# The scale of the first 128 channels as 16 single-column products on TensorE

## The chip, the cores and the metric

The kernel runs on one core of one Trainium2 chip. The metric is the device time of one execution in microseconds (us). Engines: PE is TensorE's matmul, PEld its weight load, DVE is VectorE, ACT is ScalarE, POOL is GpSimd, SP is SyncE, whose queue issues most DMAs.

## The reference

One layer of a bidirectional encoder, float32, with SEQ = 1024 positions, D = 2048 channels, batch 1. Only mixer 0, the pooling mixer, is used at this depth.

```python
m = silu(c) @ w_mod + b_mod                  # c: (1, D); shift, scale, gate of D each
shift, scale, gate = split(m, 3)
h = rms_norm(x) * (1.0 + scale) + shift
u, g = split(h @ w_in, 2)                    # w_in: (D, 2 D)
pooled = [centred_window_mean(u_i, w) - u_i  for w in (2, 4, 8, 16)]   # four groups of 512 channels
y = (pooled @ w_grp) * pool_scale
x = x + gate * ((y * silu(g)) @ w_out)
out = rms_norm(x) * final_norm_g
```

## The kernel before, in words

Activations lie with channels on partitions: x is given transposed (`xT`), so a block k of 128 channels is a tile of 128 x 1024. There are 16 such blocks, k = 0 to 15. Each large product is made from three: both operands are split into a high part in the type fp32r (`whi`, `hhi`) and a low part, the difference to it (`wlo`, `hlo`), and PE does high x high, low x high and high x low.

The first loop (lines 249 to 274) goes over k. For each k it needs three loads: 128 rows of the modulation matrix, given transposed so that output channels lie on partitions (`wm`, 1 MB), 128 rows of x (`xs`, 512 KB) and a block of weights of 128 x 512 (`wraw`, 256 KB). VectorE multiplies `wm` with SiLU(c) and sums along the row; that is the scale of these 128 channels (`mss[:, k, 1]`, after adding `b_mod` and 1, tile `bss`). For this, c is loaded as a copy over all partitions (`cB`, 128 x 2048, 1 MB), on which ScalarE does SiLU in two halves. For k = 0 to 3 the dot product is made in two halves of 1024 (`first_scale`, line 238), for later k in one (`mod_dot`, line 191). ScalarE then makes `hhi` = x times the scale (line 254; two halves for k < 4), VectorE makes `hlo` (`low_half`, line 226), and PE does 24 products of 128 x 512 into four pairs of PSUM banks `g_ps` (`first_products`, line 230). The factor of the RMS norm is applied later: ScalarE squares x (line 256), VectorE sums the squares in `acc` (`add_square`).

The order of the work is the order of the code: the schedule is written by hand, each engine works through its instructions in that order, and SP issues loads in that order. A new tile for `wm`, of which there are three buffers, waits until the last reader of its buffer is done.

Before the loop the loads go out in this order: the copy of c in two halves, `bss`, `wm` of k = 0 in two halves, `wraw` of k = 0, x of k = 0 in two halves, then `wm`, x and `wraw` of k = 1 and of k = 2. PE meanwhile does N_WARM = 30 products of a tile of ones into a bank that nobody reads (`warm`, line 219).

After the first loop come the other products with the input weights (line 170), the group products, the shift, the output products (line 878) and the closing norm. Where a sum over channels is needed, the kernel uses products with a single column of ones: 8 of them for the sum of squares (line 709) and others for the shift (`shift_sum`, line 331).

Of the kernel before, what the change touches and what calls it, by code (L numbers as in the profile page):

```python
# [8 lines left out]
F32 = mybir.dt.float32  # L9
F32R = mybir.dt.float32r  # L10
AF = mybir.ActivationFunctionType
ALU = mybir.AluOpType
PSUM = bass.MemoryType.PSUM
DRAM = bass.MemoryType.DRAM

N_WARM = 30
P = 128
D = 2048
T = 1024
NK = D // P  # L20
# [4 lines left out]


@with_exitstack
def encoder_layer(ctx, tc, xT, x, c, mod_ss, mod_g, b_ss, b_g, w_steps, wo_steps, pool_scale, edge_rcp, final_g, out):
    nc = tc.nc
    const = ctx.enter_context(tc.tile_pool(name="const", bufs=1))  # L30
    psum = ctx.enter_context(tc.tile_pool(name="psum", bufs=1, space=PSUM))
# [7 lines left out]
    bss = const.tile([P, NK, 2], F32, name="bss")  # L39
    mss = const.tile([P, NK, 2], F32, name="mss")  # L40
# [97 lines left out]
    modp = tc.alloc_tile_pool(name="modp", bufs=1, side="right")  # L138
# [4 lines left out]
    def row_tile(slot, name):  # L143
        return upool.tile([P, T + 2 * PAD], F32, tag=f"row{slot}", name=name)
# [4 lines left out]
    def load(s):  # L149
        if s < n_steps:  # L150
            w_raw[s] = wpool.tile([P, 512], F32, tag="wraw", name=f"wraw{s}")
            nc.sync.dma_start(out=w_raw[s], in_=w_steps[s])
# [22 lines left out]
    with tc.manual_schedule():  # L175

        cB = modp.tile([P, D], F32, name="cB")
        wm, xs, sq = {}, {}, {}

        def load_mod(i, k, parts=1):  # L180
            wm[i, k] = modp.tile([P, D], F32, tag="wm", bufs=3, name=f"wm{i}_{k}")
            w = D // parts
            for t in range(parts):
                nc.sync.dma_start(out=wm[i, k][:, t * w:(t + 1) * w], in_=mod_ss[i, k * P:(k + 1) * P, t * w:(t + 1) * w])
# [11 lines left out]
        def mod_bias(i, k):  # L196
            nc.vector.tensor_tensor(out=mss[:, k, i:i + 1], in0=mss[:, k, i:i + 1], in1=bss[:, k, i:i + 1], op=ALU.add)

        for t in range(2):
            nc.sync.dma_start(out=cB[:, t * 1024:(t + 1) * 1024], in_=c[:, t * 1024:(t + 1) * 1024].broadcast_to([P, 1024]))  # L200
        nc.sync.dma_start(out=bss, in_=b_ss)
        load_mod(1, 0, 2)
        load(0)
        xs[0] = row_tile(0, "x0")[:, :T]
        for t in range(2):
            nc.sync.dma_start(out=xs[0][:, t * 512:(t + 1) * 512], in_=xT[0:P, t * 512:(t + 1) * 512])
        for k in (1, 2):
            load_mod(1, k, 2)
            load_x(k)
            load(k)  # L210
        for t in range(2):
            nc.scalar.activation(cB[:, t * 1024:(t + 1) * 1024], cB[:, t * 1024:(t + 1) * 1024], AF.Silu)

        h_hi, h_lo = {}, {}

        warm, warm_in = bank_pair(3, "warm"), upool.tile([P, 512], F32R, tag="row4", name="warm_in")
        nc.vector.tensor_copy(out=warm_in.rearrange("p (a b) -> p a b", a=4), in_=ones.rearrange("p (o b) -> p o b", o=1).broadcast_to([P, 4, P]))
        for n in range(N_WARM):
            nc.tensor.matmul(warm[:, 0, :], warm_in[:, 0:P], warm_in, start=True, stop=True)
        g_ps = [bank_pair(j, f"g_ps{j}") for j in range(4)]  # L220

        def add_square(k):
# [15 lines left out]
        def first_scale(k):  # L238

            m = wm.pop((1, k))  # L240
            for t in range(2):
                a = slice(t * 1024, (t + 1) * 1024)
                nc.vector.tensor_tensor_reduce(out=m[:, a], in0=m[:, a], in1=cB[:, a], scale=1.0, scalar=0.0, op0=ALU.mult, op1=ALU.add, accum_out=mg[:, t, k:k + 1])
            if k == 0:
                nc.vector.tensor_scalar(out=bss[:, :, 1], in0=bss[:, :, 1], scalar1=1.0, scalar2=None, op0=ALU.add)
            nc.vector.scalar_tensor_tensor(out=mss[:, k, 1:2], in0=mg[:, 0, k:k + 1], scalar=mg[:, 1, k:k + 1], in1=bss[:, k, 1:2], op0=ALU.add, op1=ALU.add)

        first_scale(0)
        for k in range(NK):
            if k > 3:  # L250
                mod_bias(1, k)
            h_hi[k] = hpool.tile([P, T], F32R, tag="hi", bufs=NK, name=f"hhi{k}")
            for a in [slice(0, T)] if k > 3 else [slice(0, 512), slice(512, T)]:
                nc.scalar.activation(h_hi[k][:, a], xs[k][:, a], AF.Copy, scale=mss[:, k, 1:2])
            sq[k] = row_tile(3 + k % 2, f"sq{k}")[:, :T] if k else acc
            nc.scalar.activation(sq[k], xs[k], AF.Square)
            split_hi(k + 1)
            split_lo(k)
            if k < 3:
                low_half(k)  # L260
            add_square(k - 1)
            if k < 3:
                first_scale(k + 1)
            elif k + 1 < NK:
                mod_dot(1, k + 1)
            if k >= 3:
                low_half(k)
            if k + 3 < NK:
                load_mod(1, k + 3, 2 if k == 0 else 1)
            else:  # L270
                load_mod(0, k + 3 - NK)
            load_x(k + 3)
            load(k + 3)
            first_products(k)
# [341 lines left out]
        for s in range(NK, n_steps):  # L616
# [75 lines left out]
            if q == 0 or kind == "grp":  # L692
                name = f"{job[0]}{job[1]}_{job[2]}"
                ps = take_pair(name)
            hi, lo = w_hl.pop(s)
            for i in range(4):
                if s == sum_at and i == 2:
                    early_sum()
                a = slice(i * P, (i + 1) * P)
# [340 lines left out]
```

## Time and profile before

| | |
|---|---|
| median of 3 runs | 1136.46 us |
| lowest, highest run | 1133.23, 1136.73 us |
| profiled execution: its time | 1137.46 us |
| profiled execution: its span, first to last instruction | 1135.7 us |
| mean granted clock of TensorE | 0.993 |
| PE busy | 1118.6 us, 98% |
| PEld busy | 921.7 us, 81% |
| DVE busy | 729.8 us, 64% |
| ACT busy | 320.4 us, 28% |
| HBM read, written | 205.59 MB, 60.83 MB |

All stretches are counted from the first instruction of the span. The busy time of an engine says how full it is over the whole span; what a change in one stage is worth is read from the chain of waits and from the time line of that stage. Products are pipelined on PE: the next begins before the one ahead has ended, so the time per product is read from the starts of groups, not from the mean duration of one. In a count of a short stretch, products that only reach into it are counted too. The granted clock is 1.00 at 2.4 GHz and 0.50 at 1.2 GHz.

### The profile page before, as it was taken

Reading aid. Unit: us, or ns where it says so; the run is one execution under the profiler, and the core shown is the slowest. Engines: PE = TensorE matmul, PEld = TensorE weight load, DVE = VectorE, ACT = ScalarE, POOL = GpSimd, SP = SyncE. Lnnn points to the kernel's source line nnn. Section 1 sums busy time; section 2 is a strip of 40 time slices with the busy share of each in tenths; the row PEclk is TensorE's granted clock in tenths of the full one; section 3 lists DMA queues with packets and bytes.
Section 4 is the critical chain, followed back from the end, with each engine's and each line's share of the span. In section 5 each row is a group of like instructions: output and inputs, shape, how many; then the busy total and the mean of one; then the engine's idle time right before and its main releaser. Section 6 shows DMA issues by size and latency. Waiting matters only on the chain.

```text
span 1135.7 us, 13202 instructions
## 1 busy us (share of the span) xinstructions
PE 1118.6 (98%) x4938; PEld 921.7 (81%) x4938; DVE 729.8 (64%) x1218; ACT 320.4 (28%) x444; POOL 38.7 (3%) x79
## 2 busy tenths in 40 slices
PE   9999999999999999999999999999999999999996
PEld 7888887788888888888887888888888888888886
DVE  6996877866655566665646477634355358477795
ACT  4544110331221111222102112211235345242453
POOL 0000000000000000000000000000000010002100
PEclk9999999999999999999998999999999999999998
DMA  9995889147958977735797311123396667649954
GB/s 367 369 354 218 326 299 275 63 148 223 267 141 239 308 213 235 204 86 151 242 253 222 117 47 47 55 84 102 121 330 227 211 178 269 202 165 242 243 194 193
DMA packets 86335, 233.72 MB, mean 206 GB/s; under 512 B 9088, under 2 KB 17280, under 8 KB 82432
## 3 DMA queue, kind: packets, MB, share of 16 engines
q1 hardware_dynamic: 78464, 205.63, 51.8%
q0 software_dynamic: 7808, 27.27, 13.4%
q8 instruction: 38, 0.62, 0.2%
q14 instruction: 25, 0.20, 0.1%
HBM read 205.59 MB, written 60.83 MB: 235 GB/s over the span
## 4 chain that ended last, share of the span: by engine, by line
PE 84%; DMA 8%; DVE 6%; issue 1%; ACT 1%; SPq 0%; DVEq 0%; ACTq 0%
PE ops L878 26%; PE ps_u L170 23%; PE ps_g L170 20%; PE ps_y L170 8%; PE g_ps L235 6%; DMA gm<-in_mod_g 3%; DVE wm L194 3%; DMA early<-in_w_steps 2%; DMA wm<-in_mod_ss 1%; PE ops L972 1%; DMA wraw<-in_w_steps 1%; DMA gdram<-gr 1%; DVE wlo L162 1%; DVE early_acc L432 1%; PE vs_ps L331 0%
## 5 line engine op out<-in xcount | busy, mean ns | idle before, releaser
L162 DVE TENSOR_TENSOR wlo<-wraw,whi 128x512 fp32r<-128x512 f32 x144 | 99.2, 689 | 195.2 <-ACT whi L156 195.0
L156 ACT CAST whi<-wraw 128x512 fp32r<-128x512 f32 x144 | 89.1, 620 | 327.2 <-DMA wraw<-in_w_steps 105.8
L170 PE MATMUL ps_u<-hhi,wlo 128*128 128x512 f32 x512 | 158.4, 391 | 2.5 <-DVE wlo L162 2.5
L170 PE MATMUL ps_u<-hhi,whi 128*128 128x512 f32 x512 | 159.9, 394 | 0.0
L170 PE MATMUL ps_u<-hlo,whi 128*128 128x512 f32 x512 | 158.4, 390 | 0.0
L878 PE MATMUL ops<-wohi,zhi 128*128 128x512 f32 x432 | 133.0, 389 | 0.0
L878 PE MATMUL ops<-wohi,zlo 128*128 128x512 f32 x432 | 133.0, 389 | 0.0
L878 PE MATMUL ops<-wolo,zhi 128*128 128x512 f32 x432 | 132.9, 389 | 0.0
L170 PE MATMUL ps_g<-hhi,whi 128*128 128x512 f32 x384 | 119.9, 394 | 1.6 <-ACT whi L156 1.6
L170 PE MATMUL ps_g<-hhi,wlo 128*128 128x512 f32 x384 | 119.7, 393 | 1.2 <-DVE wlo L162 1.2
L170 PE MATMUL ps_g<-hlo,whi 128*128 128x512 f32 x384 | 119.2, 392 | 0.0
L170 PEld LDWEIGHTS ps_u<-hhi,wlo 128*128 128x128 f32 x512 | 96.2, 188 | 23.5 <-DVE wlo L162 3.3
L568 DVE TENSOR_TENSOR wolo<-woraw,wohi 128x1024 fp32r<-128x1024 f32 x56 | 68.4, 1221 | 72.7 <-ACT wohi L567 72.3
L170 PEld LDWEIGHTS ps_u<-hlo,whi 128*128 128x128 f32 x512 | 96.6, 189 | 20.4
L170 PEld LDWEIGHTS ps_u<-hhi,whi 128*128 128x128 f32 x512 | 95.7, 189 | 19.9 <-issue 0.5
L878 PEld LDWEIGHTS ops<-wohi,zhi 128*128 128x128 f32 x432 | 81.1, 188 | 16.9
L878 PEld LDWEIGHTS ops<-wolo,zhi 128*128 128x128 f32 x432 | 81.1, 188 | 16.8
L878 PEld LDWEIGHTS ops<-wohi,zlo 128*128 128x128 f32 x432 | 81.1, 188 | 16.8
L170 PEld LDWEIGHTS ps_g<-hhi,wlo 128*128 128x128 f32 x384 | 72.8, 190 | 17.0 <-DVE wlo L162 1.7
L170 PEld LDWEIGHTS ps_g<-hhi,whi 128*128 128x128 f32 x384 | 72.3, 190 | 16.8 <-ACT whi L156 2.0
L170 PEld LDWEIGHTS ps_g<-hlo,whi 128*128 128x128 f32 x384 | 72.6, 189 | 15.4
L567 ACT CAST wohi<-woraw 128x1024 fp32r<-128x1024 f32 x56 | 58.9, 1051 | 55.5 <-DVE woraw L560 27.6
(148 smaller groups left out, 1279.2 us busy)
## 6 DMA issues: line engine op xcount, KB each, us to landing
wraw<-in_w_steps SPq DMA_DIRECT2D x144, 256.0 KB, 3.9
wm<-in_mod_ss SPq DMA_DIRECT2D x28, 1024.0 KB, 7.3
wsum<-in_wo_steps SPq DMA_DIRECT2D x16, 1024.0 KB, 8.3
wsum<-in_wo_steps POOLq DMA_DIRECT2D x16, 1024.0 KB, 11.0
gm<-in_mod_g SPq DMA_DIRECT2D x32, 512.0 KB, 6.7
woraw<-wsum SPq DMA_DIRECT2D x32, 512.0 KB, 6.3
woraw<-in_wo_steps SPq DMA_DIRECT2D x32, 512.0 KB, 4.5
zraw<-zdram SPq DMA_DIRECT2D x48, 256.0 KB, 3.4
```

The lines of the kernel that those rows point to most:

```text
L156: nc.scalar.copy(out=hi, in_=w_raw[s])
L162: nc.vector.tensor_tensor(out=lo, in0=raw, in1=w_hl[s][0].bitcast(F32), op=ALU.subtract)
L170: nc.tensor.matmul(ps[:, t, :], a, b[:, t * 512:(t + 1) * 512], start=first and n == 0, stop=last and n == 2,)
L194: nc.vector.tensor_tensor_reduce(out=m, in0=m, in1=cB, scale=1.0, scalar=0.0, op0=ALU.mult, op1=ALU.add, accum_out=mss[:, k, i:i + 1])
L235: nc.tensor.matmul(g_ps[j][:, t, :], a[:, j * P:(j + 1) * P], b[:, t * 512:(t + 1) * 512], start=first and m == 0, stop=last and m == 2)
L432: nc.vector.scalar_tensor_tensor(out=early["acc"], in0=t, scalar=mss[:, k, 0:1], in1=early["acc"], op0=ALU.mult, op1=ALU.add)
L567: nc.scalar.copy(out=hi, in_=raw)
L568: nc.vector.tensor_tensor(out=lo, in0=raw, in1=hi.bitcast(F32), op=SUB)
L878: nc.tensor.matmul(ps[:, b_, :], z[:, a], w[:, q_ * 512:(q_ + 1) * 512], start=first and m == 0, stop=last and m == 2, skip_group_check=more)
L972: nc.tensor.matmul(ps[:, 0, :w], zz[:, a], ww[:, lo:lo + w], start=k == 0 and q_ == 0, stop=k == HK - 1 and q_ == 2)
```

## The change

The scale of block k = 0 is no longer made on VectorE. The modulation matrix's part for it is given once more, not transposed (`mod_first`: input channels on partitions, in 16 blocks of 128 x 128 side by side), and c as 16 columns of 128 (`c_col`). ScalarE does SiLU on the columns, PE adds up 16 products of a block with its column in the second bank of `warm`, and VectorE reads the sum from there and adds `bss`. The 30 warm-up products become 16 ahead of these and 4 behind. The loads are put in a new order, with the copy of c behind the operands of k = 0, and its SiLU moves behind the scaled rows of k = 0.

```diff
-N_WARM = 30
+N_WARM = (16, 4)
...
+        ccol = modp.tile([P, NK], F32, name="ccol")
+        nc.sync.dma_start(out=ccol, in_=c_col)
+        m0 = modp.tile([P, D], F32, tag="wm", bufs=3, name="m0")
+        for t in range(2):
+            nc.sync.dma_start(out=m0[:, t * 1024:(t + 1) * 1024], in_=mod_first[:, t * 1024:(t + 1) * 1024])
+        nc.sync.dma_start(out=bss, in_=b_ss)
+        xs[0] = row_tile(0, "x0")[:, :T]
+        nc.sync.dma_start(out=xs[0][:, 0:512], in_=xT[0:P, 0:512])
+        load(0)
+        nc.sync.dma_start(out=xs[0][:, 512:], in_=xT[0:P, 512:])
         for t in range(2):
             nc.sync.dma_start(out=cB[:, t * 1024:(t + 1) * 1024], in_=c[:, t * 1024:(t + 1) * 1024].broadcast_to([P, 1024]))
-        nc.sync.dma_start(out=bss, in_=b_ss)
-        load_mod(1, 0, 2)
-        load(0)
-        xs[0] = row_tile(0, "x0")[:, :T]
-        for t in range(2):
-            nc.sync.dma_start(out=xs[0][:, t * 512:(t + 1) * 512], in_=xT[0:P, t * 512:(t + 1) * 512])
         for k in (1, 2):
             load_mod(1, k, 2)
             load_x(k)
             load(k)
-        for t in range(2):
-            nc.scalar.activation(cB[:, t * 1024:(t + 1) * 1024], cB[:, t * 1024:(t + 1) * 1024], AF.Silu)
+        nc.scalar.activation(ccol, ccol, AF.Silu)
...
-        for n in range(N_WARM):
-            nc.tensor.matmul(warm[:, 0, :], warm_in[:, 0:P], warm_in, start=True, stop=True)
+        def warm_up(n):
+            for _ in range(n):
+                nc.tensor.matmul(warm[:, 0, :], warm_in[:, 0:P], warm_in, start=True, stop=True)
+
+        warm_up(N_WARM[0])
+        for k in range(NK):
+            nc.tensor.matmul(warm[:, 1, 0:1], m0[:, k * P:(k + 1) * P], ccol[:, k:k + 1], start=k == 0, stop=k == NK - 1)
+        warm_up(N_WARM[1])
...
-            if k == 0:
-                nc.vector.tensor_scalar(out=bss[:, :, 1], in0=bss[:, :, 1], scalar1=1.0, scalar2=None, op0=ALU.add)
...
-        first_scale(0)
+        nc.vector.tensor_scalar(out=bss[:, :, 1], in0=bss[:, :, 1], scalar1=1.0, scalar2=None, op0=ALU.add)
+        nc.vector.tensor_tensor(out=mss[:, 0, 1:2], in0=warm[:, 1, 0:1], in1=bss[:, 0, 1:2], op=ALU.add)
         for k in range(NK):
...
                 nc.scalar.activation(h_hi[k][:, a], xs[k][:, a], AF.Copy, scale=mss[:, k, 1:2])
+            if k == 0:
+                for t in range(2):
+                    nc.scalar.activation(cB[:, t * 1024:(t + 1) * 1024], cB[:, t * 1024:(t + 1) * 1024], AF.Silu)
```

The queue of SP at the start of the program, before (`wm_0`, `wm_1` are the modulation rows of k = 0 and 1, `wraw` the weights, `x` the rows of x; the numbers behind the names are those of buffers):

```order
L200 DMA cB<-in_c 128x1024 x2
L201 DMA bss<-in_b_ss 128x32
L184 DMA wm_0_123<-in_mod_ss 128x1024 x2
L152 DMA wraw_126<-in_w_steps 128x512
L206 DMA x_128<-in_xT 128x512 x2
L184 DMA wm_1_131<-in_mod_ss 128x1024 x2
L189 DMA x_134<-in_xT 128x1024
L152 DMA wraw_136<-in_w_steps 128x512
```

And now (`m` is the block for the columns, `ccol` the columns of c):

```order
L201 DMA ccol<-in_c_col 128x16
L204 DMA m_122<-in_mod_first 128x1024 x2
L205 DMA bss<-in_b_ss 128x32
L207 DMA x_126<-in_xT 128x512
L152 DMA wraw_128<-in_w_steps 128x512
L209 DMA x_126<-in_xT 128x512
L211 DMA cB<-in_c 128x1024 x2
L184 DMA wm_1_133<-in_mod_ss 128x1024 x2
L189 DMA x_136<-in_xT 128x1024
L152 DMA wraw_138<-in_w_steps 128x512
```

The copy of c went from the head of the queue to a place behind the operands of k = 0; ahead of the modulation rows of k = 1 there is one load more, of 8 KB.

ScalarE at the same place, before (`whi` is the cast of the weights, `hhi` the scaled rows, `acc` and `sq` the squares):

```order
L212 ACT_TABLE_LOAD
L212 ACTIVATE cB<-cB 128x1024 x2
L156 CAST whi_184<-wraw_126 128x512
L254 ACTIVATE hhi_190<-x_128,mss 128x512 x2
L256 ACTIVATE acc<-x_128 128x1024
L156 CAST whi_194<-wraw_136 128x512
L254 ACTIVATE hhi_234<-x_134,mss 128x512 x2
```

And now:

```order
L216 ACT_TABLE_LOAD
L216 ACTIVATE ccol<-ccol 128x16
L156 CAST whi_191<-wraw_128 128x512
L263 ACTIVATE hhi_195<-x_126,mss 128x512 x2
L266 ACTIVATE cB<-cB 128x1024 x2
L268 ACTIVATE acc<-x_126 128x1024
L156 CAST whi_201<-wraw_138 128x512
L263 ACTIVATE hhi_241<-x_136,mss 128x512 x2
```

The two SiLU passes over the copy of c stand behind the scaled rows of k = 0 now, and ahead of the square and of the cast of the weights of k = 1.

## Rows read from the trace of the kernel before

**Rows 1.** The page, part 1: busy us, share of the span, instructions.

```profile
PE 1118.6 (98%) x4938; PEld 921.7 (81%) x4938; DVE 729.8 (64%) x1218; ACT 320.4 (28%) x444; POOL 38.7 (3%) x79
```

**Rows 2.** The chain of waits, 0 to 300 us: start us, us, what.

```profile
16.09 1.34 ACT hhi L254 x2
...
31.61 1.21 DVE hlo L228
32.86 66.04 PE g_ps L235 x290
```

**Rows 3.** Time line of PE, start: start us, us, instruction, [idle before <-releaser].

```profile
7.43 0.39 PE L219 MATMUL warm<-warm_in 128*128 128x512 f32 x1
...
11.55 2.14 PE L235 MATMUL g_ps<-hhi,whi 128*128 128x512 f32 x8 [0.79 <-ACT hhi L254]
...
17.17 1.98 PE L235 MATMUL g_ps<-hhi,whi 128*128 128x512 f32 x8
...
32.86 1.43 PE L235 MATMUL g_ps<-hlo,whi 128*128 128x512 f32 x5 [0.45 <-DVE hlo L228]
```

**Rows 4.** Time line of DVE, 7 to 16 us.

```profile
7.64 1.23 DVE L243 CUSTOM_DVE_ANT_0 wm<-wm,cB 128x1024 f32<-128x1024 f32 x1 [6.24 <-DMA wm<-in_mod_ss]
...
10.52 0.22 DVE L246 SCALAR_TENSOR_TENSOR mss<-mg,bss 128x1 f32<-128x1 f32 x1
...
12.15 1.29 DVE L228 SCALAR_TENSOR_TENSOR hlo<-x,mss,hhi 128x1024 fp32r<-128x1024 f32 x1 [0.81 <-ACT hhi L254]
13.35 1.22 DVE L243 CUSTOM_DVE_ANT_0 wm<-wm,cB 128x1024 f32<-128x1024 f32 x1
...
15.76 0.22 DVE L246 SCALAR_TENSOR_TENSOR mss<-mg,bss 128x1 f32<-128x1 f32 x1
```

**Rows 5.** Time line of ACT, 4 to 18 us.

```profile
4.79 1.06 ACT L212 ACTIVATE cB<-cB 128x1024 f32<-128x1024 f32 x1 [2.77 <-DMA cB<-in_c]
6.07 1.06 ACT L212 ACTIVATE cB<-cB 128x1024 f32<-128x1024 f32 x1 [0.22 <-DMA cB<-in_c]
...
10.78 1.34 ACT L254 ACTIVATE hhi<-x,mss 128x512 fp32r<-128x512 f32 x2 [0.47 <-DVE mss L246]
...
15.56 0.62 ACT L156 CAST whi<-wraw 128x512 fp32r<-128x512 f32 x1 [2.49 <-DMA wraw<-in_w_steps]
```

**Rows 6.** Time lines of PE and ACT at the single-column products.

```profile
105.61 1.84 PE L709 MATMUL ssq_ps<-ones,acc 128*128 128x1 f32 x16
107.32 0.71 PE L170 MATMUL ps_u<-hhi,whi 128*128 128x512 f32 x2
...
202.31 1.95 PE L331 MATMUL vs_ps<-ones,early_acc 128*128 128x1 f32 x16
204.11 1.12 PE L170 MATMUL ps_u<-hhi,whi 128*128 128x512 f32 x2
...
204.29 0.23 ACT L442 COPY vcol<-vs_ps 128x4 f32<-128x4 f32 x2 [2.71 <-PE vs_ps L331]
```

**Rows 7.** Warm-up products (line 219) alone, by stretches: PE busy (count), granted clock, DMA.

```profile
1.46:6.24 4.78, 4.78 (x11) 1.00 0.92 309
1.46:7.42 5.96, 5.96 (x16) 1.00 0.93 325
```

**Rows 8.** Time line of SP's queue at the start.

```profile
0.74 0.86 SPq L200 DMA_DIRECT2D cB<-in_c  x2
```

**Rows 9.** Stretches: us, busy (count) of PE or all engines, granted clock, DMA share, GB/s.

```profile
0.00:5.00 5.00, 3.54 (x8) 2.81 (x9) 0.43 (x1) 1.50 (x2) 0.94 (x7) 1.00 0.61 199
10.00:15.00 5.00, 4.21 (x19) 3.14 (x18) 4.16 (x9) 2.60 (x4) 0.00 (x0) 1.00 1.03 404
...
108.64:112.05 3.41, 3.41 (x17) 1.00 0.98 408
...
204.21:207.62 3.41, 3.41 (x10) 0.50 0.44 152
...
603.57:610.40 6.83, 5.96 (x14) 0.50 0.82 271
```

More of the change, by code (lines that the diff above doesn't have):

```diff
@@ L27, in encoder_layer @@
 @with_exitstack
-def encoder_layer(ctx, tc, xT, x, c, mod_ss, mod_g, b_ss, b_g, w_steps, wo_steps, pool_scale, edge_rcp, final_g, out):
+def encoder_layer(ctx, tc, xT, x, c, c_col, mod_first, mod_ss, mod_g, b_ss, b_g, w_steps, wo_steps, pool_scale, edge_rcp, final_g, out):
     nc = tc.nc
@@ L1020 @@
         "c": a["c"],
+        "c_col": a["c"].reshape(NK, P).T,
+        "mod_first": w_mod[:, D:D + P].reshape(NK, P, P).transpose(1, 0, 2).reshape(P, D),
         "mod_ss": w_mod[:, :2 * D].T.reshape(2, D, D),
```

## The prediction

> **What bounds the kernel now.** I read the busy shares first, then the chain of waits over the first 300 us, then the start of the program engine by engine. PE is busy 98% of the span and VectorE 64% [rows 1]: a microsecond that PE gains or loses at the start reaches the end, as long as nothing else is what PE waits for. The chain [rows 2] says what that is. From 32.86 us PE runs 290 products of the first loop without a gap. Before that the chain is not PE, and it does not pass through the scale of the first 128 channels: it goes through the landing of the weights of k = 1 (`wraw`), the scaled rows of k = 1 on ScalarE (16.09), and VectorE's row of low halves, dots and sums for k = 1 to 4 up to the low half of k = 3 at 31.61. So the start has two things in it: when k = 0 begins on PE (11.55), and when VectorE reaches the low half of k = 3 (31.61), on which PE waits at 32.86 [rows 3]. The change works on the first; the second decides the time.
>
> How much room lies between them? In the dense stretch 290 products take 66.04 us [rows 2], 0.228 us each. From 11.55 to 32.86 [rows 3] are 21.31 us, in which PE does 24 products for each of k = 0, 1, 2 and 16 for k = 3, 88 in all, 20.0 us. The rest, 1.3 us, is waiting at k = 3 and slow first products after a wait. Even if k = 0 began earlier, PE would only wait longer at k = 1, 2 or 3.
>
> **The change, part by part.** *Removed from VectorE:* the two dot products of k = 0, 1.23 us each, the first at 7.64, and the sum that gives the scale at 10.52 [rows 4]. ScalarE then starts the scaled rows at 10.78 [rows 5], so from the scale to the rows 0.26 us, and PE begins 0.77 us later [rows 3]. VectorE had been idle for 6.24 us before these dots, so no other work moves up through their absence.
>
> *Added to PE:* 16 products of a 128x128 float32 block with one column. The same form stands twice in the trace: 8 products of it are 16 rows, two passes each, 1.71 us from 105.61 to 107.32 and 1.80 us from 202.31 to 204.11 [rows 6]. A pass is 0.113 us, so 32 passes take 3.6 us. A rule speaks for a higher price. The Trainium skill, FP8 and Floating Point Precision, section TensorE Precision Notes, states four passes for true FP32, and TensorE: Matmul & The Clock Gate, section LDWEIGHTS, one weight load of columns / 1.2 ns, 107 ns for 128 columns; an estimate from both is 16 x 4 x 107 ns = 6.8 us, and the sum below would end 3.2 us later. The rows show two records per product, and the sum goes by them.
>
> *When do they begin?* They stand behind 16 warm-up products. The seventeenth product of the warm-up began at 7.43 [rows 3, 7]. Their operands are there by then. The copy of c, which had the queue's head, was issued at 0.74, 0.43 us per half [rows 8], and its halves were used at 4.79 and 6.07 [rows 5]. The new block is as large and is issued behind one small load, that is one issue (0.44 us) later: 5.2 and 6.5 us. So: columns from 7.43, the last pass at 10.93. The last pass at 202.3 began 0.11 us before 204.11, and the copy that reads it began at 204.29, 0.29 us after that start [rows 6], so the scale is added at 11.22, and 0.26 later, at **11.48**, the scaled rows start; before it was 10.78. The scale of k = 0 comes 0.70 us **later**, not earlier, and k = 0 begins on PE at 12.25. The four warm-up products (0.9 us, to 11.95) fill the gap.
>
> *Moved on ScalarE:* the two SiLU passes over the copy of c, 1.06 us each [rows 5], now behind the scaled rows of k = 0: 11.48 + 1.25 = 12.73, 13.79, 14.85. The copy itself has 2.75 MB ahead of and in it, as the first rows of x had before; those were there by 10.78, so it is there too. The square of x, a pass of the same size, follows to 15.9, so the cast of the weights of k = 1, which began at 15.56 on their landing [rows 5], starts 0.3 us late, and the rows of k = 1 could follow it at 15.9 + 0.53 = 16.43; that matters only if nothing else is later.
>
> *VectorE after it:* from the scaled rows the low half starts 1.37 us later (10.78 to 12.15), takes 1.20, and the two dots of k = 1 end in the scale 2.41 us on (13.35 to 15.76) [rows 4]; the rows of k = 1 follow 0.25 later. From 11.48 that gives 12.85, 14.05, 16.46 and **16.71**, where it was 16.09: 0.62 us later. The second dot needs the second SiLU half at 14.85 and starts at 15.20, so this is hidden with 0.35 us to spare. The other bound on k = 1 is its weights: up to their landing the same bytes go through the queue (4.5 MB and 8 KB), one issue later: 15.56 + 0.44 + 0.53 = 16.53, below 16.71. From k = 1 on VectorE's row is unchanged, and it was the chain, so its low half of k = 3 comes at 32.15 and PE resumes at 33.48 instead of 32.86. PE, from 12.25, would be there at 32.3 without waits, 1.1 us before with a slow first product.
>
> *At nothing:* the earlier add of 1 to the bias and the other order of the first loads; each is used before 11.48 and lands before. If VectorE were not idle until 7.64 this would not be free.
>
> **Sum:** + 0.62 us. The profiled execution took 1137.46 us for a span of 1135.7; with the change 1138.1. It lies 1.0 us above the median of the runs shown, so against that median (1136.46) I say **1137.1**. A measurement of this kernel tells about 0.3% (3.4 us) from no change; its own runs span 1133.23 to 1136.73.
>
> **The rivals.**
> *1. The scale is not the bound.* The columns begin when the clock of the warm-up has risen. In this execution 11 products fill the first 4.78 us, 0.43 us each, and the others follow at 0.23 [rows 7] (the clock column has no change there, so the spacing tells it); if the clock rises 1.3 us earlier, three products more go fast and the columns begin 0.62 us earlier. Then the weights of k = 1 decide, as before, and the change does nothing: 1136.5. For it: only 0.62 us decide. Against it: nothing in this trace says when the clock will rise.
>
> *2. The clock falls over the columns.* After the 16 single-column passes at 202.3 the granted clock was 0.50 (1.2 GHz) for 3.41 us, with 10 products in that stretch; after the 16 at 105.6 it stayed at 1.00, with 17 in an equal stretch [rows 9]. Nothing in these rows says why the two differ. The change issues 32 passes in a row. A fall costs 7 products, 1.6 us. If it lies on the products of k = 0, these have 1.1 us to spare (32.3 and the slow first product, against 33.48): + 0.62 + 0.5 = + 1.1. If it takes in half of the columns, these stretch by up to 1.7 us and the scale with them: + 2.3. Middle 1138.2. By the rule of the Trainium skill, TensorE: Matmul & The Clock Gate, Part 1, the clock is throttled by default and released by activity, which speaks against putting columns into the warm-up; of the two rows one agrees and one does not.
>
> *3. Slower by over 0.3%: the columns cost twice.* The place is PE between 7.4 and 14.6 us. At the lower clock the warm-up products were spaced 0.43 against 0.23; 32 passes at that ratio take about 7 us (an estimate from these spacings), the scale comes 3.4 to 3.6 us later still, and VectorE's row with it: + 4.1, 1140.6. It decides from the point where the clock falls ahead of the columns' first half and stays low, as it did for 6.83 us at 603.57 behind waits of PE [rows 9]. Against it: 16 dense products stand directly ahead. Four passes for a float32 product (the Trainium skill, FP8 and Floating Point Precision, TensorE Precision Notes) would end at nearly the same time; the two records per product speak against it.
>
> *4. The queue runs ahead.* In the first microseconds, with the copy of c at its head, DMA moved less while it was busy: over 0 to 5 us 199 GB/s at a share of 0.61, over 10 to 15 us 404 at 1.03 [rows 9]. At the later rate per share 0.61 of 5 us would have moved 1.2 MB instead of 1.0, so 0.5 us is lost there. If that comes from the start of the copy and the new order avoids it, the weights of k = 1 land 0.5 us earlier and, with columns as early as in rival 1 and more, the whole row moves up by that: 1136.0. Beyond this there is little room, since the waits and slow starts of PE in the loop are 1.3 us in all.
>
> **How the numbers follow.** My forecast (+ 0.3 to + 1.0) 0.35, rival 1 0.25, rival 2 0.25, rival 3 0.08, rival 4 0.07. All but rival 3 lie within 0.3%. The runs of the kernel before differ among themselves by 0.31%, PE's two waits and the low clock at 600 to 611 us among the reasons I can see, so I give 0.05 to faster from that alone, 0.01 more to slower: faster 0.05, same 0.86, slower 0.09. Range: below, the lowest run of the same program, 1133.2; above, the far end of rival 2 (1138.8) and a part of that spread: 1139.6. Rival 3 is left out, and part of the scatter.
>
> **What would show it.** Right: the last column pass at about 10.9 us; the first scaled rows at 11.2 to 11.7, later than 10.78; VectorE's first dot of k = 1 directly behind the low half of k = 0; the rows of k = 1 at about 16.7; PE's wait for the low half of k = 3 ending at 33.3 to 33.6; all later stretches as before, only shifted. Rival 1 shows as rows of k = 1 at 16.1, with the cast of the weights just ahead; rival 2 as a granted clock of 0.50 and products spaced 0.43 between 9 and 17 us; rival 3 as columns that end after 14 us; rival 4 as weights of k = 1 cast before 15.2. Wrong altogether would be a gain of over 1.5 us that starts before 33 us, or a later stretch that changes its length.

## Result and profile after

The changed kernel took 1141.5 us in median (1140.98 to 1144.73), the kernel before 1136.46 (1133.23 to 1136.77): ratio 1.0056 [1.0038, 1.0074], that is 0.6% slower, and above the forecast's range (1133.2 to 1139.6). The profiled run took 1141.5 us for a span of 1139.7, 4.0 us more than the profiled span before.

The page's part 1 answers to [rows 1]: PE has 22 more instructions and is busy 0.8 us longer, so 3.2 of the 4.0 us are waiting or tail (the time from the last product to the end).

```profile
PE 1119.4 (98%) x4960; PEld 922.8 (81%) x4960; DVE 727.3 (64%) x1214; ACT 320.3 (28%) x445; POOL 38.6 (3%) x79
```

The time line of PE over the start (start us, us, instruction, wait before it) answers to [rows 3]:

```profile
1.46 5.51 PE L224 MATMUL warm<-warm_in 128*128 128x512 f32 x16 [1.46 <-DVE warm_in L221]
6.81 3.63 PE L228 MATMUL warm<-ccol,m 128*128 128x1 f32 x32
10.30 1.16 PE L224 MATMUL warm<-warm_in 128*128 128x512 f32 x4
12.46 3.78 PE L245 MATMUL g_ps<-hhi,whi 128*128 128x512 f32 x8 [1.01 <-ACT hhi L263]
16.04 3.16 PE L245 MATMUL g_ps<-hhi,wlo 128*128 128x512 f32 x8
19.04 2.01 PE L245 MATMUL g_ps<-hlo,whi 128*128 128x512 f32 x8
...
35.40 1.98 PE L245 MATMUL g_ps<-hlo,whi 128*128 128x512 f32 x8
```

The 32 passes take 3.49 us (6.81 to 10.30). They begin 0.62 us earlier than the prediction's 7.43, since the clock rose earlier in this execution: the trace's record of the granted clock begins at 4.89 us, that of before at 6.24. That is the condition of rival 1. Yet k = 0 begins at 12.46 instead of 11.55, its first eight products are busy 3.78 us instead of 2.14, and PE has no wait from there to 35.40, where before it waited until 32.86. The time lines of VectorE and ScalarE, answering to [rows 4] and [rows 5], show why k = 0 is late:

```profile
11.49 0.16 DVE L257 TENSOR_TENSOR mss<-warm,bss 128x1 f32<-128x1 f32 x1 [4.40 <-PE warm L224]
```

```profile
11.69 1.34 ACT L263 ACTIVATE hhi<-x,mss 128x512 fp32r<-128x512 f32 x2 [2.93 <-DVE mss L257]
...
15.98 0.62 ACT L156 CAST whi<-wraw 128x512 fp32r<-128x512 f32 x1
16.92 1.33 ACT L263 ACTIVATE hhi<-x,mss 128x512 fp32r<-128x512 f32 x2 [0.32 <-DVE mss L254]
```

What the scale's read waits for is line 224, the four trailing warm-up products, not line 228, the columns. Both write the tile `warm`, in different banks of one pair, and the wait is set for the tile. The last of these products ends at 11.46, 1.2 us after the columns made way for them at 10.30. And the row of that stretch (us, busy and count per engine, clock, DMA) shows the granted clock at 0.50, the 1.2 GHz level, for 6.83 us:

```profile
11.71:18.54 6.83, 6.08 (x14) 4.80 (x15) 5.20 (x9) 6.40 (x9) 0.00 (x0) 0.50 1.02 410
```

Against before, product by product, PE is 0.91 us late at the first product of k = 0, 3.7 at the end of the slow ones and 2.41 at the first product of k = 4 (37.21 against 34.81), since the waits of before that end at 28.47 and 32.86 are no longer there. From there two things are added which the prediction did not have. Between 312 and 447 us PE loses 1.47 us, nearly all of it in a wait that before does not have (time line of PE):

```profile
422.11 0.70 PE L170 MATMUL ps_u<-hhi,whi 128*128 128x512 f32 x2 [1.02 <-DVE g L350]
```

And 9.44 us instead of 9.01 lie between the start of the last product and the end of the span. The waits of SyncE over the last 10 us (engine, line, waited for, us, times, longest) differ, first the changed kernel, then before:

```profile
SPq L1050 <- DMA out<-r: 3.0, 1, 3.0
```

```profile
SPq L1036 <- DMA out<-r: 2.6, 2, 1.3
```

At the end of the program SyncE waits in turn for the completion semaphores that its loads and stores use in rotation. Before, the semaphores of the last two stores are the last two in turn. The changed kernel issues one load more, the turn is shifted by one, and behind the last landing SyncE still goes through the seven other waits, long satisfied, 0.06 us each.

2.41 at the start, 1.47 around 422 us and 0.43 at the end, less 0.2 between 100 and 210 us and 0.1 near 600 us, are the 4.04 us. That the two stages in the middle come out so near to before's is chance, as their scatter over all profiles tells (under e8): before has a low clock at 204 and 604 us [rows 9], the changed kernel only for 3.41 us from 609.05, and its waits of PE there are longer instead (near 600 us 4.0 us against 2.8).

### The profile page after: what moved, and what is told of

The parts are those of the page before. It is cut to its first block, busy times and chain, and to the rows that moved or that the text cites. A ratio compares the mean times of both kernels' runs of the same rounds, so it can differ in the third digit from the quotient of the medians.

```text
span 1139.7 us, 13245 instructions
## 1 busy us (share of the span) xinstructions
PE 1119.4 (98%) x4960; PEld 922.8 (81%) x4960; DVE 727.3 (64%) x1214; ACT 320.3 (28%) x445; POOL 38.6 (3%) x79
## 4 chain that ended last, share of the span: by engine, by line
PE 81%; DMA 11%; DVE 5%; issue 1%; ACT 1%; SPq 0%; POOL 0%; DVEq 0%; ACTq 0%; POOLq 0%
PE ops L890 26%; PE ps_u L170 22%; PE ps_g L170 16%; PE g_ps L245 8%; PE ps_y L170 7%; DMA gm<-in_mod_g 6%; DMA early<-in_w_steps 2%; DVE wm L194 2%; DMA wm<-in_mod_ss 1%; PE ops L984 1%; DMA gdram<-gr 1%; DMA wraw<-in_w_steps 1%; PE warm L224 1%; DVE early_acc L444 1%; DVE wlo L162 1%
## 6 DMA issues: line engine op xcount, KB each, us to landing
wsum<-in_wo_steps POOLq DMA_DIRECT2D x16, 1024.0 KB, 10.1
```

## Experiments

The theories. **Tile:** the trailing warm-up products hold the scale back. **Clock:** the columns let the clock fall. **Later waits:** they come from one of three things: the place of the two added inputs in memory (*layout*), the one load more (*count*), or c's copy behind the first operands (*order*).

All kernels, each against before on the same chip. k = 0 and k = 4: start of their first product in the profile (before 11.55 and 34.81). 420: what the profile gains between 312 and 447 us on before's. Tail: from the start of the last product to the end. Clock: (1 - mean granted clock) x span, the clock's share, mean over the runs (before 5.9 to 6.6 us); the rest is the span less this. The share is no pure loss: it also counts the low clock behind the last product, where PE has nothing to do (in before's profile from 1129.2 us to the end, 3.2 us of share), and it leaves out the slow products before the clock first rises. A single profile's k = 4 is not exact either: the other four kernels that make the scale as before, with eight loads (e3, e5, e8, e10), have it 0.1 to 0.65 us behind that profile of before.

| kernel | median us | ratio | k = 0 | k = 4 | 420 | tail | clock |
|---|---|---|---|---|---|---|---|
| changed | 1141.5 | 1.0056 [1.0038, 1.0074] | 12.46 | 37.21 | +1.47 | 9.44 | 9.8 |
| e1_own_bank | 1140.65 | 1.0041 [1.0027, 1.0055] | 11.77 | 35.57 | +0.95 | 9.45 | 8.7 |
| e2_dense | 1137.73 | 1.0019 [1.001, 1.0028] | 12.23 | 35.58 | +2.80 | 9.44 | 5.4 |
| e3_cols_in_before | 1137.59 | 1.0024 [1.0008, 1.004] | 11.67 | 35.29 | 0.00 | 9.00 | 9.5 |
| e4_mixed | 1141.84 | 1.0059 [1.0034, 1.0083] | 15.03 | 37.44 | +0.75 | 9.44 | 6.5 |
| e5_inputs_only | 1138.86 | 1.0017 [1.0005, 1.0029] | 12.16 | 35.46 | +0.15 | 9.00 | 6.3 |
| e6_one_more_load | 1136.84 | 1.0011 [1.0, 1.0022] | 13.73 | 38.19 | 0.00 | 9.43 | 7.0 |
| e7_eight_loads | 1138.37 | 1.0028 [1.0008, 1.0048] | 11.94 | 35.73 | +0.25 | 9.00 | 8.1 |
| e9_inputs_last | 1139.39 | 1.0031 [1.0014, 1.0047] | 15.16 | 39.53 | 0.00 | 9.44 | 9.1 |
| e10_inputs_last_only | 1135.09 | 0.9994 [0.9984, 1.0005] | 11.64 | 34.90 | 0.00 | 9.01 | 6.0 |
| e11_all_three | 1137.03 | 1.0008 [0.9997, 1.002] | 11.39 | 35.44 | 0.00 | 9.02 | 8.2 |
| e12_groups | 1137.51 | 1.0014 [1.0004, 1.0025] | 15.70 | 38.42 | 0.00 | 9.01 | 8.0 |
| e13_wide64 | 1137.4 | 1.0019 [1.0007, 1.0032] | 11.66 | 35.35 | 0.00 | 8.99 | 7.1 |
| e14_wide128 | 1136.49 | 1.0016 [1.0004, 1.0027] | 12.84 | 36.01 | 0.00 | 9.01 | 6.3 |
| e15_same_bank | 1140.65 | 1.004 [1.0026, 1.0055] | 15.16 | 39.51 | 0.00 | 9.00 | 10.1 |
| e16_dense_repaired | 1137.59 | 1.002 [1.0011, 1.003] | 11.73 | 35.45 | 0.00 | 9.01 | 7.0 |
| e17_after_again | 1142.81 | 1.0046 [1.0028, 1.0064] | 15.16 | 39.40 | +1.49 | 9.43 | 10.5 |
| e18_repaired_again | 1138.14 | 1.0016 [1.0003, 1.0028] | 13.94 | 37.40 | 0.00 | 9.00 | 8.9 |

e8, a second profile of before, has k = 0 at 11.60, k = 4 at 35.17, 0.00 at 420, tail 9.01.

**e1_own_bank.** The trailing products write a pair of banks of their own.

```diff
+        spare = bank_pair(2, "spare")
-        warm_up(N_WARM[1])
+        warm_up(N_WARM[1], spare)
```

> The four warm-up products behind the columns write to another pair of banks, so that the scale on VectorE need not wait for them. Theory A (the clock): the scale is read at about 10.6 us instead of 11.49 and k = 0 begins on PE at about 11.6, but the granted clock still falls to 0.50 behind the columns, PE is dense from k = 0 on and reaches the low-half products of k = 3 at 34.5 to 35; time 1139 to 1141, at most 1 us below the changed kernel. Theory B (the late scale): the loss at the start goes away, these products start at 32.9 to 33.2, time 1136.5 to 1137.5.

The scale's read now waits for the columns (VectorE), and PE goes from the spare products to k = 0 without a wait (PE):

```profile
10.80 0.16 DVE L259 TENSOR_TENSOR mss<-warm,bss 128x1 f32<-128x1 f32 x1 [3.27 <-PE warm L230]
```

```profile
7.14 3.63 PE L230 MATMUL warm<-ccol,m 128*128 128x1 f32 x32
10.62 1.17 PE L226 MATMUL spare<-warm_in 128*128 128x512 f32 x4
11.77 2.14 PE L247 MATMUL g_ps<-hhi,whi 128*128 128x512 f32 x8
```

The tile dependence is shown: from the last pass (10.51) to the read 0.29 us, as the prediction took it, and k = 4 only 0.76 us late. The clock did not fall in this execution. The total hardly moved, and 3.0 of this profile's 3.8 us come after k = 4, so most of the loss stands elsewhere.

**e2_dense.** 16 dense products (512 columns each) in place of the columns; the kernel leaves out the scale of k = 0.

```diff
-            nc.tensor.matmul(warm[:, 1, 0:1], m0[:, k * P:(k + 1) * P], ccol[:, k:k + 1], ...)
+            nc.tensor.matmul(warm[:, 1, :], warm_in[:, 0:P], warm_in, start=True, stop=True)
```

> The 16 column products are replaced by 16 warm-up products of 512 columns, which take the same 3.6 us; the scale of the first 128 channels is then not computed (it is a constant plus its bias), everything else is as in the changed kernel, the late scale at 11.5 too. Theory A (the clock): no stretch of 0.50 before 100 us, k = 0 begins at about 12.4, the low-half products of k = 3 at 33.5 to 33.9, time 1137 to 1138. Theory B (the late scale): they start at 35.4 and the time is 1141 as in the changed kernel. Theory C (the new order of the loads makes later waits longer): start as in theory A, but PE's waits after 100 us as long as in the changed kernel, time 1139 to 1140.

No fall of the clock at the start in the profile, and the clock's share is below before's, though the scale waits for the trailing products as in the change (1.01 us on PE at 12.23). Without a fall, that wait leaves k = 4 no later than banks of their own do (0.77 us, e1 0.76). Half the loss is left, with waits of 1.00 and 1.26 us at 408 and 414.

**e3_cols_in_before.** The columns alone, on data at hand, in the kernel before; nothing reads them.

```diff
-        for n in range(N_WARM):
+        for n in range(16):
...
+        for k in range(NK):
+            nc.tensor.matmul(warm[:, 1, 0:1], ident, ones[:, 0:1], start=k == 0, stop=k == NK - 1)
+        for n in range(4):
```

> The kernel before, with its 30 warm-up products replaced by 16 of them, 16 single-column products on the identity that nobody reads, and 4 warm-up products; scale on VectorE and order of loads as before. Theory A (the clock): a stretch of 0.50 that begins between 8 and 13 us, k = 0 at 11.55 as before, the low-half products of k = 3 at 34 to 35.5 instead of 32.86, time 1138 to 1140.5. Theories B and C: 1136.5, as the kernel before.

The clock falls with the columns alone, here from 11.76 for 3.41 us (busy and count per engine, clock, DMA):

```profile
11.76:15.17 3.41, 3.41 (x8) 2.66 (x9) 2.90 (x4) 1.42 (x2) 0.00 (x0) 0.50 1.03 410
```

The runs are 2.8 us slower in mean span (standard error 0.9) and their clock's share is 3.6 us higher (0.8). In this profile the fall costs only 0.5 us at k = 4. The later waits of the change, 420 and tail, are not there.

**e4_mixed.** A dense product between every two columns, 9 warm-ups ahead and 8 behind.

```diff
+            if k < NK - 1:
+                warm_up(1, spare)
```

> The changed kernel with 9 warm-up products ahead, one dense product of 512 columns between every two column products, and 8 behind, those in another pair of banks. The scale comes later than in the changed kernel (columns and dense products take about 7 us from 5.3: read at about 12.5). Theory A (the clock): the clock stays at 1.00 from its rise on, the low-half products of k = 3 start at about 34.7 because VectorE's row is 1.9 us late, time about 1138.4. Theory B (the late scale): later than the changed kernel by the 1 us by which the scale is later still, 1142.

The clock holds, but the columns now end at 13.1 us and k = 0 begins at 15.03: the cure costs at least what it saves.

**e5_inputs_only, e10_inputs_last_only.** The kernel before with the two added inputs, unread: in e5 in the middle of the list, as in the change, in e10 at its end.

```diff
         "c": a["c"],
+        "c_col": a["c"].reshape(NK, P).T,
+        "mod_first": w_mod[:, D:D + P].reshape(NK, P, P)...,
```

> The kernel before with the two added inputs (c_col, 8 KB, and mod_first, 1 MB) in the list of inputs and nothing else: no load of them, no products. In every kernel so far that has the new loads the waits of TensorE after 100 us are 8.5 to 9.9 us in sum and 9.4 us lie behind the last product; in before and in columns-in-before 4.6 to 6.4 and 9.0. Layout theory (the inputs behind them lie at other addresses of the memory, so the loads of later stages take longer): waits of 8 to 10 us in sum, over 3 us near 600 us, 9.4 us behind the last product, 1137.5 to 1138.5. Count theory (one load more ahead of k=1's) and order theory (c behind the first operands): as before, 1135 to 1136.5, waits of 4.5 to 6.5 us.

> The kernel before with the two added inputs at the end of the list, unread: the control to the same with them in the middle (1138.9, rest 1130.4). Layout theory: as before, 1136 to 1137, rest 1128 to 1128.6. If it is the number of inputs and not their place: 1138 to 1139, rest about 1130.4.

The program is that of before in both. With the inputs in the middle the span is 1.9 us above before's in mean, at the end 0.5 below it: 2.4 us (standard error 0.7) for the place of 1 MB that nothing reads. Where they arise is not shown: of the 2.1 us that e5's profile loses, 0.15 lie at 420, the others at the start and in the two stages with waits, which scatter in any case.

**e9_inputs_last.** The same move in the change.

> The change, with its two added inputs at the end of the list of inputs instead of in the middle, so that the inputs of before keep their places. Each run gives its span and its mean granted clock; (1 - clock) x span is called the clock's share here, the remainder the rest. Layout theory (the kernel before with the added inputs in the middle had a rest 2.2 us above before's, 1130.4 against 1128.2): the rest falls by some 2 us from the change's 1130.8 to about 1129, and the median to 1139 to 1140; the clock's share stays at 8 to 10 us (before 5.9 to 6.6). If the place of the inputs is nothing: 1141 to 1142, rest 1130.8, as the change.

The rest is 1128.5 against 1130.8 in the change and 1129.8 in the change measured again (e17, below): 1.3 to 2.3 us less, which is the way of the layout theory, but by itself hardly clear of the scatter. The wait at 420 is gone; in the same place VectorE's dot on the gate's weights waits less for its load, first the change, then e9:

```profile
417.80 1.23 DVE L610 CUSTOM_DVE_ANT_0 gm<-gm,c_half 128x1024 f32<-128x1024 f32 x1 [5.55 <-DMA gm<-in_mod_g]
```

```profile
416.66 1.22 DVE L610 CUSTOM_DVE_ANT_0 gm<-gm,c_half 128x1024 f32<-128x1024 f32 x1 [4.71 <-DMA gm<-in_mod_g]
```

SyncE issued these loads at 411.67 and 411.38, so the first took 0.85 us longer to its use. Over all profiles the column 420 divides by the inputs alone: seven with the megabyte in the middle gain 0.15 to 2.80 us there, the thirteen without (before itself among them) 0.00. The order theory falls by this: e9 and e11 keep the new order and gain nothing there. That other addresses are the reason is argued, not shown; no run shows them.

**e6_one_more_load, e7_eight_loads.** Count theory: e6 is before with the 8 KB load at the head, unread; e7 is e1 with the new block in one load instead of two.

> The kernel before with one load more at the head of the program, the 8 KB of c_col, which nothing reads; no products, c in its old place. Count theory (each load of the program moves one place on in the round of completion semaphores, so that later waits of SyncE are joined to other loads): the later waits of the change appear, 8 to 10 us in sum after 100 us, 3 us near 600 us, 9.4 us behind the last product, and 1137.5 to 1138.5. Order theory (c's copy behind the first operands moves the phase of the loads): as before, 1135 to 1136.5, waits of 4.5 to 6.5 us after 100 us, 9.0 us behind the last product. Layout theory: 8 KB shift the inputs behind by a little; as before or the half.

> The change with the trailing warm-up products in banks of their own and the 1 MB of the first modulation weights loaded in one piece in place of two, so that eight loads, as before, stand ahead of those of k=1. Count theory: later waits as before (4.5 to 6.5 us after 100 us in sum, 9.0 us behind the last product), 1136 to 1137.5. Order and layout theories: as the kernel with its own bank, 8.5 to 10 us in sum, 9.4 us behind the last product, 1139.5 to 1141.

Count sets the tail: 9.43 to 9.45 us in the seven profiles with nine loads, 8.99 to 9.02 in the thirteen with eight. The 420 wait does not follow it. e6 shows by the way that columns are not needed for a fall. Its 30 dense warm-up products end 3.3 us before the products of k = 0 can begin, and the clock was low from 12.44 for 6.83 us (PE's time line):

```profile
13.73 3.78 PE L237 MATMUL g_ps<-hhi,whi 128*128 128x512 f32 x8 [3.26 <-ACT hhi L256]
```

**e8_before_again.** Before, word for word.

> The kernel before, word for word, for a second profile of it. If its later waits differ from one execution to the next by chance, the sum after 100 us lies anywhere from 4.5 to 10 us and that near 600 us from 1.8 to 3.5; if they belong to the program, 4.5 to 6.5 in sum, 1.8 near 600 and 9.0 behind the last product, as in the first profile.

The waits of PE after 100 us sum to 4.6 us (first profile 5.3, the change 8.4), 3.3 of them near 600 us (2.8 and 4.0). Among all profiles the stage of 100 to 210 us differs from before's by - 3.5 to + 2.5 us and that near 600 us by - 1.4 to + 1.1, so no reading here rests on them. Their waits also take up part of what is lost at the start: e12 is 3.6 us late at k = 4 and 0.1 at 212 us.

**e11_all_three, e18_repaired_again, e17_after_again.** The repairs together (own banks, inputs last, eight loads), twice, and the change again beside the second.

> The change with the three repairs together: trailing warm-up products in banks of their own, the added inputs last, eight loads ahead of k=1's. The columns stay as they are. If these three are all that is lost besides the clock, the rest is before's plus the 0.4 to 0.8 us of the start (1128.5 to 1129), the clock's share that of the other kernels with columns (8 to 9.5 us), in all 1138 to 1139.5 in median. If the rest stays at 1130 or above, something else of the new order costs.

> The kernel with the three repairs, word for word. If the repairs give the loss back: 1136.5 to 1138, ratio 0.9995 to 1.0025, that is 2.5 to 4.5 us below the change on the same chip, the start 0.5 to 0.9 us behind before's whether the clock falls there or not. If the repaired kernel's first result was chance: 1139 or above.

> The change, word for word, on the chip of the repaired kernel. If the loss belongs to the program: 1139.5 to 1141.5, ratio 1.003 to 1.006, the last products of the first low half 2.4 to 4.7 us later than in before, 9.4 us behind the last product, waits at 420 and over 2.9 us near 600 us. If it was the chip of the first runs: 1136 to 1138.

The loss belongs to the program, and the repairs give 3.9 us of mean span back on the same chip (standard error 1.0). What is left, 0.9 and 1.8 us by the ratios, has intervals that take in the forecast's 0.62. The scale is then no bound, as e11's PE shows:

```profile
6.76 3.63 PE L229 MATMUL warm<-ccol,m 128*128 128x1 f32 x32
10.25 1.19 PE L225 MATMUL spare<-warm_in 128*128 128x512 f32 x4
11.39 3.65 PE L246 MATMUL g_ps<-hhi,whi 128*128 128x512 f32 x8
```

Its ScalarE begins the rows of k = 0 at 10.61, earlier than before (10.78). But the weights of k = 1 land so late that their cast waits until 16.18 (before 15.56), and the rows of k = 1 follow the cast:

```profile
10.61 1.34 ACT L264 ACTIVATE hhi<-x,mss 128x512 fp32r<-128x512 f32 x2 [2.11 <-DVE mss L258]
...
16.18 0.62 ACT L156 CAST whi<-wraw 128x512 fp32r<-128x512 f32 x1 [1.39 <-DMA wraw<-in_w_steps]
16.71 1.33 ACT L264 ACTIVATE hhi<-x,mss 128x512 fp32r<-128x512 f32 x2
```

In e17 and e18 the clock fell earlier, first e17, then e18:

```profile
7.59 4.64 PE L228 MATMUL warm<-ccol,m 128*128 128x1 f32 x32
12.10 2.05 PE L224 MATMUL warm<-warm_in 128*128 128x512 f32 x4
15.16 3.78 PE L245 MATMUL g_ps<-hhi,whi 128*128 128x512 f32 x8 [1.01 <-ACT hhi L263]
```

```profile
7.89 4.33 PE L229 MATMUL warm<-ccol,m 128*128 128x1 f32 x32
12.09 2.05 PE L225 MATMUL spare<-warm_in 128*128 128x512 f32 x4
13.94 3.61 PE L246 MATMUL g_ps<-hhi,whi 128*128 128x512 f32 x8
```

Where the clock falls among them, the columns stretch to 4.2 to 4.5 us, and from the start of the four trailing products to that of k = 0 lie 1.85 us (e18) instead of 1.14 (e11). In the change these products are on the scale's path: in e17 the clock was low from 9.98 for 10.24 us, and k = 0 began at 15.16. With banks of their own they are not: in e18 it was low for 6.83 us, k = 0 began at 13.94.

**e15_same_bank.** The repaired kernel with the trailing products in the columns' tile again.

> The kernel with the three repairs but without the first: the trailing warm-up products write the columns' tile again, so that the scale waits for them. Dependence theory: the scale's read comes 0.7 to 1.1 us later, TensorE has a wait of about 1 us ahead of the first step's products, and the median is 1137.7 to 1139.5 (with a larger clock's share, since the wait lies behind the columns). If that wait is covered by later waits for loads: 1137, as with banks of their own.

Mean span 4.1 us above before's, against 1.1 and 2.0 for the kernels with own banks: the dependence costs 2 to 3 us (standard error about 1), more than the wait of 1.2 us that it sets. The profiles go with a longer fall: k = 4 is at 39.51 here and the clock low from 10.16 for 10.24 us. Where the clock had risen at nearly the same time, the kernel with the wait has the longer fall each time: risen at 4.7 to 5.0 us, 6.83 us of low clock (changed) against 3.41 (e3, e11); risen at 6.5 to 7.3 us, 10.24 (e9, e15, e17) against 6.83 (e18).

**e12_groups.** Columns in four groups of four, one dense product between groups, after 10 warm-ups.

> The same repairs, and the columns in four groups of four with one dense product between two groups, started after 10 warm-up products in place of 16 (x of the first step in one load, so that eight loads remain). Clock theory: the pauses in dense work become short, the clock's share goes back to 6 to 7 us, and with a rest of 1128.5 to 1129 the median is 1136 to 1137, as before or 0.3 us either side. If any columns cost clock, however they are spread: clock's share 8 to 9.5 us, 1138 to 1139.5. The columns' end is at about 10.3 us as in the change, the rows of the first step at 10.7.

A miss: the columns began at 5.88 and, with the dense products between them, ran until 13.85, at 0.20 us per pass instead of 0.11. This is the spacing of the low clock (the four trailing products take 1.85 us, as in e18 at the low clock), and the trace's record of the granted clock begins only at 17.7 us. So in this execution the clock had not risen ahead of the columns, and the theory was not put to the test.

**e13_wide64, e14_wide128, e16_dense_repaired.** The repaired kernel with 64 or 128 equal columns per product, or dense products instead.

```diff
-            nc.tensor.matmul(warm[:, 1, 0:1], ..., ccol[:, k:k + 1], ...)
+            nc.tensor.matmul(warm[:, 1, 0:128], ..., ccol[:, k:k + 1].broadcast_to([P, 128]), ...)
```

> The kernel with the three repairs, each product of the columns with 64 equal columns of c (broadcast) in place of one. If the clock falls because each weight load is given one column only: the clock's share falls from 8.2 towards 6 to 7 us, and if the products stay as long as they are (0.226 us each, bound by the weight loads) the median is 1135 to 1136, at or below before's. If the clock's share stays at 8 us: 1137, as with single columns. If the products get longer (64 columns at two records each), 0.05 to 0.1 us each more, the start is 1 to 1.5 us later.

> The same with 128 equal columns. One-column theory: clock's share 6 to 6.5 us, as in kernels without columns; the products 0.226 to 0.43 us each, 16 of them 3.6 to 6.8 us, so the start up to 3 us later; 1135 to 1138 by that. If weight loads in close order are themselves what lets the clock fall, the share stays at 8 us: 1137 to 1140.

> The kernel with the three repairs, with 16 dense warm-up products in place of the columns; the first 128 channels' scale is not computed (its dot product is left out). Clock theory: the clock's share is 5.4 to 6.6 us, as in kernels without columns; these products take 2.7 to 3 us longer than the columns, so the start is 1 to 2.5 us later, partly taken up by waits that follow; rest 1127.5 to 1129, median 1135 to 1137. If the clock's share stays at 8 us, it is not the columns but the order of the loads that costs clock.

128 columns take no longer than one (PE's time line of e14), and the clock does not fall behind them in this execution:

```profile
8.10 3.73 PE L229 MATMUL warm<-ccol,m 128*128 128x128 f32 x32
11.59 1.17 PE L225 MATMUL spare<-warm_in 128*128 128x512 f32 x4
12.84 2.14 PE L246 MATMUL g_ps<-hhi,whi 128*128 128x512 f32 x8
```

But the total does not follow: mean span 1.4 to 2.2 us above before's for the three, 1.1 and 2.0 for single columns. On the repaired base a fall of the clock and its absence cannot be told apart in the time, and the clock's share divides them only weakly: over before's it is 0.2 (e14) to 1.0 us (e13) higher with wide columns and 1.7 (e11) and 2.7 (e18) with single ones, each with a standard error of 0.5 to 0.7. That wide columns keep the clock up is therefore likely, not shown. No version beat the kernel before.

## Why the prediction was wrong

- **The columns' price: right.** 3.49 us for 3.6 forecast, two records per product. The 6.8 us that the prediction worked out with the four passes of the Trainium skill (FP8 and Floating Point Precision, TensorE Precision Notes) did not come; whether a record holds more than one pass, no run shows.
- **"so the scale is added at 11.22": failed.** The step took the last pass of the columns as the end of the wait and let the four trailing products "fill the gap". The tile that the scale reads is theirs too, so they lay on the path: the scale was read at 11.49 in the change, 1.2 us after the columns' end, although the columns had begun 0.62 us early; in e1, with banks of their own, 0.29 us after the last pass. By itself this wait costs nothing that shows at k = 4 (e2 against e1). With the fall of the clock that follows, the dependence costs 2 to 3 us (e15 against e11 and e18).
- **Rival 1, the scale is not the bound: its condition came, its result did not.** The columns began 0.62 us early, as it supposes, but the tile wait and the low clock took this back and more.
- **Rival 2, the clock: happened, and was priced too low.** It had + 1.1 to + 2.3 by a fall of 3.41 us that costs 7 products, 1.6 us. The fall lasted 6.83 us in the first profile of the change and 10.24 in the second, with k = 4 late by 2.41 and 4.6 us, both with the tile wait in it. In the second the low clock also stretched the trailing products, which the forecast did not have on the path. By the Trainium skill, TensorE: Matmul & The Clock Gate, Part 1, the clock is released by activity. The runs agree so far as single columns go: it fell behind them in 7 of 9 profiles with the columns in one row, for 3.4 to 10.2 us, and in none of the five with dense products, 64 or 128 columns, or a dense product between every two columns. But the moment counts too: the two that did not fall (e1, e7) had risen at 5.6 and 5.9 us, the seven at 4.7 to 5.0 or 6.5 to 7.3, the five at 4.3 to 7.7. So it is e3's runs that show the columns as a cause, not the count of profiles.
- **Weights of k = 1, "one issue later", + 0.44: sized too low, and ranked wrongly.** They were to stay below the scale's row. In e1, e7 and e11 they were cast at 16.31, 16.46 and 16.18 against 15.56, 0.6 to 0.9 us later (though e8, before once more, has 15.92), and the rows of k = 1 followed this cast, not the scale. In the change the cast (15.98) followed the square on ScalarE, and the rows of k = 1 waited for the scale (16.92).
- **"all later stretches as before, only shifted": failed**, and the prediction named a later stretch that changes its length as what would make it wrong. It looked for costs only where instructions changed. The two inputs, declared in the middle of the list, cost 2.4 us (e5 against e10) without an instruction; the one load more cost 0.43 us at the very end.
- **The + 0.62 itself: met without the tile wait, by luck.** In e1, e7 and e11 k = 4 is 0.6 to 0.9 us late, but by the weights of k = 1 and not by the scale, from which the sum had it; with a longer fall of the clock (e18) it is 2.6. With the repairs the ratio is 1.0008 [0.9997, 1.002] and 1.0016 [1.0003, 1.0028], where + 0.62 us is 1.0005. An earlier scale brought no gain: in e11 the rows of k = 0 began 0.17 us ahead of before's, and k = 4 was 0.64 us late. And in e1, with k = 0 at 11.77, PE still waits, by the spacing of its products, 0.6 us ahead of 29.23 and again ahead of 33.62; in before these waits are 0.4 and 0.6.

The parts, 2.4 for the inputs' place, 2 to 3 for the dependence with the clock, 0.4 for the tail, 0.9 to 1.8 for what is left, sum to 5.7 to 7.6 us; the ratios of the change, 1.0056 and 1.0046, are 6.4 and 5.2. The parts were measured on different bases and with standard errors of 0.6 to 1 us, so that they agree within these is all that can be said.

## What to carry to other kernels

Filler work should not write the tile that a result is read from, even in another bank: in this kernel the reader waited for the last writer of the tile. A small edit can cost as much where it has no instruction, by inputs placed ahead of others or by the count of loads that decides which semaphore is waited for last; so add an input at the end of the list, and run the unread input as a control.

## Of the hardware, not expected

- 16 products of a 128x128 float32 block take 3.49 us at the high clock with one moving column (changed) and with 128 (e14), 0.22 us each. The mean clock's share over the runs is 8.0 to 10.5 us in the ten kernels with single columns in rows of four or sixteen, and 5.4 to 7.1 in all others that ran several times, before included.
- An unread 1 MB input declared ahead of the weights made the same program 2.4 us slower than the same input declared last (e5 against e10, standard error 0.7).
- Which semaphore the last store has is worth 0.43 us at the end of the program: 9.43 to 9.45 us from the last product in seven profiles, 8.99 to 9.02 in thirteen.
